# The memory's 1/rms row read back four steps later, and the memory's four parts split in the first four merged tiles instead of every second one

## The chip, the cores and the metric

The kernel runs on one core of a Trainium2 chip. The metric is the time of one execution on the device in microseconds (us), lower is better. The core's engines work side by side, each through its own queue in order: PE (TensorE, matmuls; its weight loads, PEld, overlap them), DVE (VectorE), ACT (ScalarE), POOL (GpSimd, which also issues some DMAs) and SP (SyncE, which only issues DMAs). They wait for one another through semaphores, and an instruction that waits holds up all that is queued behind it on its engine.

## The reference

One layer of a hybrid decoder over x of 512 tokens by 1024 channels, in float32, with 256 fixed memory tokens, cut to what matters here:

```
h = rms_norm(x);  proj = h @ w_in        # q, k, v | u, gate_b, gate_c | g_a, g_b
o_a = stick_breaking_attention(q, k, v)  # 8 heads of 64, causal
y_b = gate_b * causal_depthwise_conv(gate_c * u)
merged = sigmoid(g_a) * (o_a @ w_branch_a) + sigmoid(g_b) * (y_b @ w_branch_b)
x = x + merged @ w_mix_out
x = x + memory_cross_attention(rms_norm(x), rms_norm(mem), w_mem_q, w_mem_kv, w_mem_o)
x = x + (silu(gate) * up) @ w_ffn_out    # gate, up = rms_norm(x) @ w_ffn_in
out = rms_norm(x)
```

The change touches how `rms_norm(mem)` is made. Each memory token is scaled by its own 1/rms (256 numbers) and each channel by the gain `norm_mem_kv`.

## The kernel before

**Form of the work.** Activations are kept transposed, 128 channels on the partitions and 512 tokens along the free dimension, in 8 tiles. Every float32 operand of a matmul is split into a high part (a cast to fp32r) and a low part (the value minus that cast), and a product is three matmuls, high by high, high by low and low by high (`mm3`, lines 154 to 156). So each 128x1024 weight tile (`load_w`, lines 136 to 151) is loaded by SP into one of four buffers `wr`, cast by ACT to `wh` (line 149) and subtracted by DVE to `wl` (line 150). The same is done to activations (`split`, lines 168 to 178: the cast on ACT at line 172, the rest on DVE at line 174). A product over 1024 channels is 24 matmuls into one of two PSUM banks of the pool `pmm`; the next product but one needs the same bank, and so waits until DVE has read it.

**The stages around the change.** (1) The values are projected. (2) A loop of 17 turns (lines 553 to 573) does the attention of 4 head pairs p by 4 key tiles kt = 3, 2, 1, 0, so turn i is step (p, kt) = (i // 4, 3 - i % 4). In turn i PE does one or two projections out of a list `fill`, the scores of step i+1 (`scores`, midway in a projection), the weights of step i (`weights`) and the values of step i-1 (`values`). Within the scores of a step, ACT and DVE make the softplus `e`, POOL masks its diagonal block (`causal`, the affine select at line 402), and `lsplit` splits it into two tiles `l` (cast at line 416, rest at line 417). Within the weights, PE adds the running sums of the earlier key tiles onto the bank `z` (line 480) and the own step's sums (line 483, it reads both tiles `l`), ACT exponentiates `z` into `a` (line 485), POOL masks `a` (line 402 again), and DVE splits `a` into `ah` and `al` (lines 489 and 490). At the end of a head pair (kt = 0) ACT and DVE join its output `ot` (lines 510 and 511). (3) The merged tiles, m = 0 to 7 (lines 608 to 632): two gate projections, each read by DVE with line 353, two branch products `br` of 12 matmuls each read by line 625, and the split of the merged tile into `mh` and `ml`. (4) The memory's keys `km` and values `vm` (lines 635 to 663), the output projection with the residual, the cross-attention, the FFN.

**The memory.** In turns 1, 3, 5 and 7 four pieces of the memory are squared and summed. In turn 9 `mem_factors` (lines 528 to 537) makes the 1/rms `rm` of the 256 tokens, POOL writes it to DRAM (`rmd`, line 534), and POOL reads it back as a row broadcast to all partitions (`rmb`, line 536). `rmb` is first used by the keys (line 641), in stage 4. The memory itself, transposed, is split in four parts of 256 channels by `mem_split` (lines 596 to 606): SP loads a part `mk` (line 516), ACT makes two tiles `mgh` of 128x256 (line 603) and DVE two tiles `mgl` (line 604). The parts use the pool `xpool` of 8 buffers, which the residual tiles `x` (line 697) use after them. `mem_split` is called in the merged tiles m = 0, 2, 4 and 6.

**Other work at the same time.** From the merged tile m = 1 on, POOL forms sums of FFN weights (`weight_sums`, lines 579 to 590: loads `pre`, adds with line 587, stores `sums`).

**What sets the order.** The program is recorded in the order of the Python code and a scheduler orders the instructions of each engine, so that the queues differ somewhat from the code. `after(i, earlier)` ties an instruction behind earlier ones in that order only; it adds no wait on the chip. `exps` is the list of ACT's exponentials, so `exps[-1:]` in turn i is the one that the weights of the turn before issued last.

Of the kernel before, what the change touches and what calls it, by code (L numbers as in the profile page):

```python
# [8 lines left out]
F32 = mybir.dt.float32  # L9
# [4 lines left out]
P = 128  # L14
D = 1024
S = 512
KD = D // P
# [4 lines left out]
MEM = 256  # L22
# [6 lines left out]
EPS = 1e-6  # L29
MEM_AT = (1, 3, 5, 7)  # L30
MEAN_AT = 9
EARLY = 2
WARM = 8
FIRST = 4
# [9 lines left out]
def hybrid_layer(ctx: ExitStack, tc: tile.TileContext, xT_d, memT_d, mem_d, cols_d, wv_d, win_d,  # L44
                 wbr_d, wmix_d, wmq_d, wmk_d, wmv_d, wmo_d, wfi_d, wfo_d, gfin_d, out):
    nc = tc.nc

    cpool = ctx.enter_context(tc.tile_pool(name="cpool", bufs=1))
# [14 lines left out]
    def nm(s):  # L63
        count[0] += 1
        return f"{s}{count[0]}"

    def unit(s, cols=512):
        return upool.tile([P, cols], F32R, tag="u", name=nm(s), padded_shape=[P, 512])
# [34 lines left out]
    exps, casts, lead, lows, loads = [], [], [], [], []  # L103

    def after(i, earlier):
        for e in earlier:
            tc.add_manual_dep(i.ins, e.ins.name, mybir.DependencyInfo(
                mybir.DependencyClass.NoSync, mybir.DependencyReason.DATA), reason="order")
# [7 lines left out]
    def rstd_of(var, n, s, tables=()):  # L116

        def new(t):
            return tmp(t, n) if n > TT else spool.tile([P, n], F32, tag=t, name=nm(t))

        v, y, a = new("rv"), new("ry"), new("ra")
        r = cpool.tile([P, n], F32, tag=s, name=nm(s))
        after(nc.scalar.activation(y, var, AF.Ln, bias=eps_t), tables)
        nc.vector.tensor_scalar(out=v, in0=var, scalar1=EPS, scalar2=None, op0=ALU.add)
        exps.append(nc.scalar.activation(y, y, AF.Exp, scale=-0.5))
        nc.vector.tensor_tensor(out=a, in0=y, in1=y, op=ALU.mult)
        nc.vector.scalar_tensor_tensor(out=a, in0=a, scalar=-0.5, in1=v, op0=ALU.mult,
                                       op1=ALU.mult)
        nc.vector.scalar_tensor_tensor(out=r, in0=a, scalar=1.5, in1=y, op0=ALU.add, op1=ALU.mult)
        return r  # L130
# [171 lines left out]
    def settle_behind(*last):  # L302
        while urgent or behind:
            (urgent or behind).pop(0)(*last)
# [123 lines left out]
    def scores(p, kt):  # L428
        c0, n = span(kt)
        keys = slice(kt * P, (kt + 1) * P)  # L430
        zs[p, kt] = []
        for hs in heads_of(kt):
            bank = ztile("z")
            zs[p, kt].append(bank)
            for i, h in enumerate(hs):
                for part in range(2):
                    nc.tensor.matmul(bank[:, i * n:(i + 1) * n], ks[p][h][:, keys],
                                     qs[p][h][part][:, c0:], start=i + part == 0, stop=part == 1,
                                     skip_group_check=True)
        for hs, bank in zip(heads_of(kt), zs[p, kt]):  # L440
            w = len(hs) * n
            z = bank[:, :w]
            e = tmp("e")[:, :w]
            nc.scalar.activation(e, z, AF.Abs)
            nc.scalar.activation(e, e, AF.Exp, scale=-1.0)
            nc.scalar.activation(e, e, AF.Ln, bias=1.0)
            nc.vector.scalar_tensor_tensor(out=e, in0=z, scalar=0.0, in1=e, op0=ALU.max,
                                           op1=ALU.add)
            causal(by_head(e, n))
            urgent.append(lambda *last, e=e, hs=hs: fails(p, kt, hs, e, n, last))  # L450
# [21 lines left out]
    def weights(p, kt):  # L472
        c0, n = span(kt)
        av[p, kt] = {}
        for hs, bank in zip(heads_of(kt), zs[p, kt]):
            w = len(hs) * n
            z = bank[:, :w]
            if kt < TT - 1:
                for part in carried(p, kt, hs):
                    nc.tensor.matmul(by_head(z, n)[:, :, P:], neg1, part, start=False, stop=False,  # L480
                                     skip_group_check=True)
            for part in sp[p, kt, hs]:
                nc.tensor.matmul(z, negtri, part, start=False, stop=True, skip_group_check=True)
            a = tmp("a")[:, :w]
            exps.append(nc.scalar.activation(a, z, AF.Exp))
            causal(by_head(a, n))
            ah, al = unit("ah")[:, :w], unit("al")[:, :w]
            r = r0[:, kt:kt + 1]
            nc.vector.tensor_scalar(out=ah, in0=a, scalar1=r, scalar2=None, op0=ALU.mult)
            als.append(nc.vector.scalar_tensor_tensor(out=al, in0=a, scalar=r, in1=f(ah),  # L490
                                                      op0=ALU.mult, op1=ALU.subtract))
            for h in hs:
                av[p, kt][h] = part_of((ah, al), hs, (h,), n)
# [21 lines left out]
    def load_mem(k2, t):  # L515
        nc.sync.dma_start(t, memT_d[2 * k2 * P:(2 * k2 + 2) * P, :].rearrange("(j p) t -> p j t",
                                                                              p=P))
# [3 lines left out]
    def mem_square(i):  # L521

        h, t = divmod(i, MT)
        mk = f(unit("mk"))
        nc.sync.dma_start(mk, mem_d[t, :, h * 512:(h + 1) * 512])
        nc.scalar.activation(mk, mk, AF.Square, scale=D ** -0.5, accum_out=ms[:, i:i + 1])

    def mem_factors():

        var = spool.tile([P, MT], F32, tag="mv", name="mv", bufs=1)  # L530
        nc.vector.tensor_tensor(out=var, in0=ms[:, :MT], in1=ms[:, MT:], op=ALU.add)
        rm = rstd_of(var, MT, "rm")
        d = dpool.tile([1, MEM], F32, tag="rm", name="rmd")
        nc.gpsimd.dma_start(d.rearrange("o (t p) -> p (o t)", p=P), rm)
        rmb = cpool.tile([P, MEM], F32, tag="rmb", name="rmb")
        nc.gpsimd.dma_start(rmb, d.broadcast_to([P, MEM]))
        return rm, rmb

    fill = []
    for p in range(TT):  # L540
        if p + 1 < TT:
            fill += [(qk_part, p + 1, 0), (qk_part, p + 1, 1)]
        fill += [(conv, p, i) for i in range(3)]
    for m in range(EARLY):
        fill += [(gate, m, 0), (gate, m, 1)]
# [7 lines left out]
    for i in range(len(steps) + 1):  # L553
        if i in MEM_AT:
            mem_square(MEM_AT.index(i))
        if i == MEAN_AT:
            rm, rmb = mem_factors()
        some = []
        while fill and (i == len(steps) or len(some) < (2 if steps[i][1] == 1 else 1)):
            some.append(fill.pop(0))  # L560
        if i + 1 < len(steps):
            to = lambda: scores(*steps[i + 1])
            if len(some) == 1:
                midway.append(to)
            else:
                some.insert(len(some) // 2, (to,))
        for g, *args in some:
            g(*args)
        if i < len(steps):
            weights(*steps[i])  # L570
        if i > 0:
            values(*steps[i - 1])
        settle_behind(*exps[-1:], *joined[-1:])
# [22 lines left out]
    def mem_split(k2):  # L596
        mk = xpool.tile([P, 2, MEM], F32, tag="x", name=nm("mk"))
        load_mem(k2, mk)
        his, los = unit("mgh"), unit("mgl")
        for j in range(2):  # L600
            k = 2 * k2 + j
            hi, lo = (u[:, j * MEM:(j + 1) * MEM] for u in (his, los))
            nc.scalar.activation(hi, mk[:, j, :], AF.Copy, scale=g_kv[:, k:k + 1])
            nc.vector.scalar_tensor_tensor(out=lo, in0=mk[:, j, :], scalar=g_kv[:, k:k + 1],
                                           in1=f(hi), op0=ALU.mult, op1=ALU.subtract)
            mg.append((hi, lo))
# [3 lines left out]
    for m in range(KD):  # L610
        sig = []
        for j in range(2):
            if (m, j) not in gates:
                gate(m, j)
            t = gates.pop((m, j))
            sigmoid = nc.scalar.activation(t, t, AF.Sigmoid)
            after(sigmoid, exps[-2:])
            sig.append(t)
        w = load_w(wbr_d[m])
        for j in (1, 0):  # L620
            if m == 0 and j == 0:
                gate(EARLY, 0)
            ps = mmtile("br")
            gemm(ps, w, (oT, yb)[j], 4 * j)
            nc.vector.tensor_tensor(out=sig[j], in0=ps, in1=sig[j], op=ALU.mult)
        nc.vector.tensor_tensor(out=sig[0], in0=sig[0], in1=sig[1], op=ALU.add)
        if m < KD - 1:
            merged.append(split(sig[0], "m"))
        if m == SUMS_AT:
            weight_sums(range(SUMS_FIRST), merged[m][0])  # L630
        if m % 2 == 0:
            mem_split(m // 2)


    km = []
# [796 lines left out]
```

## Time and profile before

| what | value |
| --- | --- |
| median of 3 runs | 852.82 us (852.49 to 852.87) |
| the profiled execution's own time | 852.06 us |
| its span, from the first to the last instruction | 850.4 us |
| mean granted TensorE clock | 0.996 of full speed |
| busy: PE, DVE, ACT, POOL | 99%, 77%, 53%, 18% of the span |

A profile is one execution. Rows of a timeline start with the start and the duration in us, then engine, line, operation, what is written and read (buffer numbers left out) and the shape; in square brackets stand the idle time of the engine just before and what ended it. Durations of matmuls overlap, so their pace is read from start to start. A busy PE need not be at full speed: the column PEclk of the windows view is the clock that the throttle granted.

### The profile page before, as it was taken

What the parts mean: (1) busy time and instruction counts of PE and PEld (TensorE: products, weight loads), DVE (VectorE), ACT (ScalarE), POOL (GpSimd) and SP (SyncE); (2) the same over time, 40 slices, a digit from 0 to 9 for tenths busy, and PEclk for the clock granted to TensorE, in tenths of its full rate; (3) what the DMA queues carried; (4) which work ended last, traced back from release to release, by engine and by line L of the source; (5) the groups of instructions that cost most, each with busy time, mean ns of one, the idle gap of its engine ahead of it and who ended that gap; (6) DMA issues with size and microseconds to landing.
All of it is one profiled execution on the core that took longest, in us unless ns stands there. A gap on an engine that the chain in (4) does not pass through costs nothing.

```text
span 850.4 us, 12675 instructions
## 1 busy us (share of the span) xinstructions
PE 839.1 (99%) x4779; PEld 739.7 (87%) x4779; DVE 651.5 (77%) x1037; ACT 453.5 (53%) x806; POOL 155.1 (18%) x165
## 2 busy tenths in 40 slices
PE   9999998999999999999999999999999999999996
PEld 7888887888888889888888889999999999988885
DVE  7778878885766686578555688888888888899886
ACT  7566766565333254534444565655555555666654
POOL 0011121110465650065000010211111110000301
PEclk9999999999999999999999999999999999999999
DMA  8452453225587765566441324776776773465552
GB/s 298 149 168 99 124 109 97 75 75 173 210 307 291 291 250 185 173 239 237 131 124 49 88 74 142 191 187 175 183 188 177 190 191 91 145 219 205 177 183 99
DMA packets 51359, 143.73 MB, mean 169 GB/s; under 512 B 5761, under 2 KB 7041, under 8 KB 48482
## 3 DMA queue, kind: packets, MB, share of 16 engines
q1 hardware_dynamic: 41650, 107.89, 38.2%
q0 software_dynamic: 9360, 34.75, 15.6%
q8 instruction: 37, 0.61, 0.3%
q10 hardware_dynamic: 288, 0.28, 0.1%
q14 instruction: 24, 0.20, 0.1%
HBM read 125.20 MB, written 13.64 MB: 163 GB/s over the span
## 4 chain that ended last, share of the span: by engine, by line
PE 97%; DVE 1%; issue 1%; ACT 0%; POOL 0%; DVEq 0%; POOLq 0%
PE z L856 15%; PE p L1125 12%; PE y L856 7%; PE pr L154 7%; PE pr L155 7%; PE pr L156 7%; PE v L856 4%; PE r L154 3%; PE r L156 3%; PE r L155 3%; PE v L272 3%; PE mq L154 2%; PE mq L156 2%; PE mq L155 2%; PE br L154 2%; PE br L155 2%
## 5 line engine op out<-in xcount | busy, mean ns | idle before, releaser
L149 ACT CAST wh<-wr 128x1024 fp32r<-128x1024 f32 x84 | 88.0, 1052 | 159.2 <-issue 66.1
L150 DVE TENSOR_TENSOR wl<-wr,wh 128x1024 fp32r<-128x1024 f32 x84 | 111.5, 1330 | 37.9 <-ACT wh L149 37.6
L154 PE MATMUL pr<-xgh,wh 128*128 128x512 f32 x288 | 113.4, 394 | 0.0
L155 PE MATMUL pr<-xgl,wh 128*128 128x512 f32 x288 | 112.8, 392 | 0.0
L156 PE MATMUL pr<-xgh,wl 128*128 128x512 f32 x288 | 112.7, 391 | 0.0
L587 POOL TENSOR_TENSOR pre<-pre 128x512 f32<-128x512 f32 x44 | 71.2, 1622 | 31.1 <-DMA pre<-in_w_ffn_out_dram 28.8
L825 POOL DMA_DIRECT2D ws<-in_w_ffn_in_dram x22 | 26.6, 1209 | 256.6 <-DVE wf L846 123.5
L856 PE MATMUL z<-xdh,wf 128*128 128x256 f32 x352 | 70.4, 283 | 0.0
L156 PEld LDWEIGHTS pr<-xgh,wl 128*128 128x128 f32 x288 | 54.4, 189 | 11.7
L154 PEld LDWEIGHTS pr<-xgh,wh 128*128 128x128 f32 x288 | 54.6, 189 | 10.8
L155 PEld LDWEIGHTS pr<-xgl,wh 128*128 128x128 f32 x288 | 54.5, 189 | 10.5
L877 ACT COPY sa<-z 128x256 f32<-128x256 f32 x44 | 16.4, 372 | 81.5 <-PE z L856 81.5
L856 PEld LDWEIGHTS z<-xdh,wf 128*128 128x128 f32 x352 | 58.0, 192 | 0.0
L846 DVE TENSOR_TENSOR wf<-s,wf 128x512 fp32r<-128x512 f32 x44 | 30.4, 691 | 25.7 <-ACT wf L845 25.3
L856 PE MATMUL z<-xdl,wf 128*128 128x256 f32 x176 | 49.8, 283 | 0.0
L937 DVE TENSOR_TENSOR wl<-wr,wh 128x1024 fp32r<-128x1024 f32 x33 | 41.0, 1242 | 4.8 <-ACT wh L1004 4.7
L1004 ACT CAST wh<-wr 128x1024 fp32r<-128x1024 f32 x33 | 34.6, 1050 | 5.5 <-PE xt L1210 2.8
L856 PE MATMUL v<-xoh,wf 128*128 128x256 f32 x176 | 35.4, 283 | 0.0
L856 PE MATMUL y<-xch,wf 128*128 128x256 f32 x176 | 35.4, 283 | 0.0
L856 PE MATMUL z<-xf,wf 128*128 128x256 f32 x264 | 35.4, 283 | 0.0
L856 PE MATMUL z<-xch,wf 128*128 128x256 f32 x176 | 35.3, 283 | 0.0
L856 PE MATMUL y<-xoh,wf 128*128 128x256 f32 x176 | 35.3, 283 | 0.0
(346 smaller groups left out, 2389.4 us busy)
## 6 DMA issues: line engine op xcount, KB each, us to landing
wr<-in_w_in_dram SPq DMA_DIRECT2D x36, 512.0 KB, 3.4
pre<-in_w_ffn_out_dram POOLq DMA_DIRECT2D x11, 1024.0 KB, 8.0
sums<-pre POOLq DMA_DIRECT2D x11, 1024.0 KB, 4.8
ws<-in_w_ffn_in_dram SPq DMA_DIRECT2D x22, 512.0 KB, 3.7
wg<-in_w_ffn_in_dram SPq DMA_DIRECT2D x22, 512.0 KB, 4.7
ws<-in_w_ffn_in_dram POOLq DMA_DIRECT2D x22, 512.0 KB, 6.1
wr<-sums SPq DMA_DIRECT2D x22, 512.0 KB, 3.9
wr<-in_w_ffn_out_dram SPq DMA_DIRECT2D x16, 512.0 KB, 3.6
```

Of the source, the lines that this page charges most:

```text
L149: after(nc.scalar.copy(h2, raw), lead[-1:])
L150: lows.append(nc.vector.tensor_tensor(out=l2, in0=raw, in1=f(h2), op=ALU.subtract))
L154: nc.tensor.matmul(ps, a[0], b[0], start=start, stop=False, **kw)
L155: nc.tensor.matmul(ps, a[0], b[1], start=False, stop=False, **kw)
L156: nc.tensor.matmul(ps, a[1], b[0], start=False, stop=stop, **kw)
L587: nc.gpsimd.tensor_tensor(out=t[:, a, :], in0=t[:, a, :], in1=t[:, b, :], op=ALU.add)
L825: nc.gpsimd.dma_start(s13, a[:, 0:4:3, :], accum_op=ALU.add)
L846: nc.vector.tensor_tensor(out=w[:, 1, :], in0=raw, in1=f(w[:, 0, :]), op=ALU.subtract)
L856: nc.tensor.matmul(ps[:, :HS], a, b, start=i < 3 and k == 0 and j == 0, stop=k == KP - 1 and j == 2, skip_group_check=True)
L937: nc.vector.tensor_tensor(out=lo, in0=src, in1=f(hi), op=ALU.subtract)
L1004: nc.scalar.copy(hi, raw)
L1125: nc.tensor.matmul(res[i][s2], a[:, ts], b, start=j == 0 and n == 0, stop=n == 2 and j == (BEHIND - 1 if (i, s2) == (5, 1) else NJ - 1))
```

## The change

The read-back of `rmd` into `rmb` leaves `mem_factors` and is issued in turn 13, tied behind the last exponential of turn 12. `mem_split` is called in the merged tiles m = 0, 1, 2 and 3. Both parts are kept as they are in what they compute. The short name of the change also speaks of a running sum in two parts of 128 rows; no line of the diff touches a running sum.

```diff
+ROW_AT = 13
...
         nc.gpsimd.dma_start(d.rearrange("o (t p) -> p (o t)", p=P), rm)
-        rmb = cpool.tile([P, MEM], F32, tag="rmb", name="rmb")
-        nc.gpsimd.dma_start(rmb, d.broadcast_to([P, MEM]))
-        return rm, rmb
+        return rm, d
...
         if i == MEAN_AT:
-            rm, rmb = mem_factors()
+            rm, rmd = mem_factors()
+        if i == ROW_AT:
+            rmb = cpool.tile([P, MEM], F32, tag="rmb", name="rmb")
+            after(nc.gpsimd.dma_start(rmb, rmd.broadcast_to([P, MEM])), exps[-1:])
...
-        if m % 2 == 0:
-            mem_split(m // 2)
+        if m < KD // 2:
+            mem_split(m)
```

How the queues stand before and after the change is shown at three places; a row is a line of the kernel, the operation and what it writes and reads, and the lines of the changed kernel are one or two higher. PE's own queue holds the same instructions in the same order. First POOL, in the attention of the third head pair (p = 2): `e` and `a` are the masks of softplus and weights. Before:

```order
L402 AFFINE_SELECT a_1259<-a_1259 128x128
L534 DMA rmd<-rm_1374 128x2x1
L402 AFFINE_SELECT e_1310<-e_1310 128x2x128
L536 DMA rmb<-rmd 128x256
L402 AFFINE_SELECT a_1332<-a_1332 128x256
L402 AFFINE_SELECT e_1410<-e_1410 128x128
```

The same place in the changed kernel:

```order
L403 AFFINE_SELECT a_1259<-a_1259 128x128
L535 DMA rmd<-rm_1374 128x2x1
L403 AFFINE_SELECT e_1310<-e_1310 128x2x128
L403 AFFINE_SELECT a_1332<-a_1332 128x256
L403 AFFINE_SELECT e_1408<-e_1408 128x128
```

The read-back no longer stands between the mask of `e` and the mask of `a`. It stands at the same place of the fourth head pair (p = 3), again in POOL's queue of the changed kernel:

```order
L403 AFFINE_SELECT a_1646<-a_1646 128x128
L403 AFFINE_SELECT a_1657<-a_1657 128x128
L403 AFFINE_SELECT e_1696<-e_1696 128x2x128
L559 DMA rmb<-rmd 128x256
L403 AFFINE_SELECT a_1721<-a_1721 128x256
L403 AFFINE_SELECT e_1780<-e_1780 128x128
```

It was moved past 12 masks, and waits for the same store of `rmd` as before.

Second DVE in the merged tiles 1 and 2, from the split of merged tile 1 (`ml_2196`) to the read of the next gate. Before:

```order
L626 TENSOR_TENSOR g_1995<-g_1995,g_2054 128x512
L150 TENSOR_TENSOR wl_2384<-wr_2381,wh_2383 128x1024
L174 TENSOR_TENSOR ml_2196<-g_1995,mh_2195 128x512
L353 TENSOR_TENSOR g_2297<-pr_2272,r0b_363 128x512
L150 TENSOR_TENSOR wl_2418<-wr_2415,wh_2417 128x1024
```

In the changed kernel:

```order
L628 TENSOR_TENSOR g_1995<-g_1995,g_2054 128x512
L151 TENSOR_TENSOR wl_2392<-wr_2389,wh_2391 128x1024
L175 TENSOR_TENSOR ml_2196<-g_1995,mh_2195 128x512
L606 SCALAR_TENSOR_TENSOR mgl_2268<-mk_2265,gcol,mgh_2267 128x256 x2
L354 TENSOR_TENSOR g_2305<-pr_2280,r0b_363 128x512
L151 TENSOR_TENSOR wl_2426<-wr_2423,wh_2425 128x1024
```

A pair of `mgl` now stands ahead of the gate's read; the same holds after the split of merged tile 3.

Third DVE in the merged tiles 6 and 7, where `ml_2780` before and `ml_2788` now split merged tile 6. Before:

```order
L353 TENSOR_TENSOR g_2822<-pr_2797,r0b_363 128x512
L150 TENSOR_TENSOR wl_2938<-wr_2935,wh_2937 128x1024
L174 TENSOR_TENSOR ml_2780<-g_2707,mh_2779 128x512
L604 SCALAR_TENSOR_TENSOR mgl_2786<-mk_2783,gcol,mgh_2785 128x256 x2
L353 TENSOR_TENSOR g_2856<-pr_2831,r0b_363 128x512
L150 TENSOR_TENSOR wl_2973<-wr_2970,wh_2972 128x1024
```

In the changed kernel:

```order
L354 TENSOR_TENSOR g_2822<-pr_2797,r0b_363 128x512
L151 TENSOR_TENSOR wl_2938<-wr_2935,wh_2937 128x1024
L175 TENSOR_TENSOR ml_2681<-g_2608,mh_2680 128x512
L175 TENSOR_TENSOR ml_2788<-g_2715,mh_2787 128x512
L354 TENSOR_TENSOR g_2856<-pr_2831,r0b_363 128x512
L151 TENSOR_TENSOR wl_2973<-wr_2970,wh_2972 128x1024
```

The pair of `mgl` is gone from there, and the scheduler has moved the split of merged tile 5 (`ml_2681`) down to this place.

On ACT the pairs of `mgh` moved with the pairs of `mgl`. On SP the loads of the parts `mk` stand side by side, one weight load is now behind the third of them and not ahead of it, and the loads of the last three residual tiles `x`, which take over buffers of the parts, stand earlier: by two, six and ten weight loads.

## The prediction

> **What bounds the kernel now.** I read the page's engine totals first (busy us, share of the span, instructions).
>
> ```profile
> PE 839.1 (99%) x4779; PEld 739.7 (87%) x4779; DVE 651.5 (77%) x1037; ACT 453.5 (53%) x806; POOL 155.1 (18%) x165
> ```
>
> PE is busy for 99% of the span and so the bound from end to end; a change that leaves PE's matmuls alone can only win what PE waits, or what PE does at less than full clock. The second view is the waits of PE alone (line, what it waited for, total us, times, longest).
>
> ```profile
> PE z L483 <- DVE l L417: 2.4, 1, 2.4
> PE warm L232 <- DVE neg L91: 1.4, 1, 1.4
> PE br L154 <- DVE g L353: 0.3, 1, 0.3
> ```
>
> Three waits in the whole span; the one for `neg` is the start and is not touched. The third view is the windows around the first wait (length, then busy us and count of each engine; the 1.00 or 0.50 behind POOL's is the granted clock).
>
> ```profile
> 7.20:130.60 123.40, 123.40 (x579) 103.66 (x577) 98.51 (x161) 80.38 (x149) 16.84 (x33) 1.00 0.51 152
> 130.66:133.01 2.35, 0.00 (x0) 0.00 (x0) 2.25 (x5) 0.74 (x2) 0.00 (x0) 1.00 0.82 206
> 133.44:136.88 3.44, 3.44 (x12) 2.86 (x11) 3.23 (x6) 3.44 (x9) 0.08 (x1) 0.50 0.35 81
> 137.00:846.00 709.00, 705.86 (x4177) 628.41 (x4175) 543.39 (x858) 364.48 (x643) 136.97 (x123) 1.00 0.55 172
> ```
>
> The clock is full everywhere between 7.2 and 846 us except in the 3.44 us right behind this wait, where it is 0.50. So the wait costs more than its 2.35 us.
>
> The fourth view says why PE waited: POOL's timeline.
>
> ```profile
> 120.92 0.73 POOL L534 DMA_DIRECT2D rmd<-rm  x1 [3.39 <-DVE rm L129]
> 122.90 0.40 POOL L402 TENSOR_SCALAR_AFFINE_SELECT e<-e 128x256 f32<-128x256 f32 x1 [1.25 <-DVE e L447]
> 129.13 0.57 POOL L536 DMA_DIRECT2D rmb<-rmd  x1 [5.84 <-DMA rmd<-rm]
> 129.72 0.42 POOL L402 TENSOR_SCALAR_AFFINE_SELECT a<-a 128x256 f32<-128x256 f32 x1
> ```
>
> POOL stood 5.84 us in front of the read-back until the store of `rmd` had landed, and the mask of `a` stood behind it. ACT's and DVE's timelines give what that held.
>
> ```profile
> 123.58 0.38 ACT L485 ACTIVATE a<-z 128x256 f32<-128x256 f32 x1
> ```
>
> ```profile
> 123.71 1.23 DVE L150 TENSOR_TENSOR wl<-wr,wh 128x1024 fp32r<-128x1024 f32 x1 [0.17 <-ACT wh L149]
> 130.17 0.35 DVE L489 TENSOR_SCALAR ah<-a,r 128x256 fp32r<-128x256 f32 x1 [5.23 <-POOL a L402]
> ...
> 132.26 0.69 DVE L417 TENSOR_TENSOR l<-e,l 128x512 fp32r<-128x512 f32 x1
> ```
>
> `a` was ready at 123.58 + 0.38 = 123.96, but masked only at 130.14. DVE idled 5.23 us for it, with `l`, which has nothing to do with the memory, queued behind `ah`; and PE waited for `l`.
>
> **The read-back, moved four turns on.** Its price is read from start to start on PE, against the same step of the next head pair, which has the same matmuls and no wait.
>
> ```profile
> 130.04 0.40 PE L480 MATMUL z<-l,neg 128*128 128x256 f32 x2
> 130.27 0.39 PE L483 MATMUL z<-l,negtri 128*128 128x512 f32 x1
> 133.01 0.50 PE L483 MATMUL z<-l,negtri 128*128 128x512 f32 x1 [2.35 <-DVE l L417]
> ...
> 136.99 0.39 PE L155 MATMUL pr<-xgl,wh 128*128 128x512 f32 x1
> ```
>
> ```profile
> 170.48 0.40 PE L480 MATMUL z<-l,neg 128*128 128x256 f32 x2
> ...
> 173.24 0.39 PE L155 MATMUL pr<-xgl,wh 128*128 128x512 f32 x1
> ```
>
> From the first `z` of line 480 to the eighth projection matmul it took 136.99 - 130.04 = 6.95 us here and 173.24 - 170.48 = 2.76 us there. The difference, **4.19 us**, is the wait (2.35 us), the slow stretch (half of 3.44 us, 1.72), and the drained pipeline (about 0.1).
>
> Does the wait go altogether, and what is late next? Without the read-back the mask of `a` can run at 124.0 and end by 124.5; then DVE's 1.23 us `wl`, which ends at 124.94, is the later. From the start of `ah` to the end of `l` DVE needs 132.95 - 130.17 = 2.78 us, so `l` would be done at 127.7. PE needs it one matmul after 130.27, at 130.50. That is 2.8 us to spare, so I count the whole 4.19 us. Bounds: nothing, if DVE should lose those 2.8 us and the wait's length again elsewhere; at most 4.19, since PE at full pace has no more to give here.
>
> In its new place the read-back waits for a store that landed some 35 us earlier, so only its issue counts, 0.57 us. It stands between the masks of `e` and `a` of the next head pair; the row is that of `a`:
>
> ```profile
> 164.46 0.51 POOL L402 TENSOR_SCALAR_AFFINE_SELECT a<-a 128x256 f32<-128x256 f32 x1 [0.73 <-ACT a L485]
> ```
>
> POOL is idle there for 0.73 us, which holds the 0.57. If the issue took the 0.73 of the store's, the mask would be late by under 0.1 us, and the step has about the time to spare that I have just worked out for its twin. I take 0, between 0 and 0.1. The row is first read by the keys, behind all eight merged tiles. The store itself stays where it was, and the mask of `e` behind it.
>
> **The memory's parts, moved to tiles 0 to 3.** What goes is the third wait. The rows are DVE's and PE's in merged tile 7.
>
> ```profile
> 300.09 1.78 DVE L174 TENSOR_TENSOR ml<-g,mh 128x512 fp32r<-128x512 f32 x1
> 301.80 3.37 DVE L604 SCALAR_TENSOR_TENSOR mgl<-mk,gcol,mgh 128x256 fp32r<-128x256 f32 x2
> 305.09 0.68 DVE L353 TENSOR_TENSOR g<-pr,r0b 128x512 f32<-128x512 f32 x1
> ```
>
> ```profile
> 305.11 0.39 PE L156 MATMUL br<-yh,wl 128*128 128x512 f32 x1
> 305.82 0.50 PE L154 MATMUL br<-oh,wh 128*128 128x512 f32 x1 [0.32 <-DVE g L353]
> 306.16 0.40 PE L155 MATMUL br<-ol,wh 128*128 128x512 f32 x1
> ```
>
> The gate's bank is read only after the pair of `mgl`, and the second `br` product needs that bank. At the pace of 0.23 us two matmuls take 0.46; here they took 306.16 - 305.11 = 1.05, so this costs **0.59 us**, with no fall of the clock. In the changed queue the split of tile 5 takes the pair's place. At tile 6's own pace (301.80 - 300.09 = 1.71 us, start to start) two of them end at 303.5, and the gate's read is done by 304.2, 1.1 us before PE wants the bank at 305.34. I count 0.59, between 0 (the read as late as now) and 0.59.
>
> What comes: pairs of `mgl` and `mgh` in tiles 1 and 3. DVE's rows: the pair of tile 0, the split of tile 1 with the gate's read behind it, and the same read behind the split of tile 3.
>
> ```profile
> 213.41 0.88 DVE L604 SCALAR_TENSOR_TENSOR mgl<-mk,gcol,mgh 128x256 fp32r<-128x256 f32 x2
> ...
> 218.25 0.68 DVE L174 TENSOR_TENSOR ml<-g,mh 128x512 fp32r<-128x512 f32 x1
> 221.22 0.69 DVE L353 TENSOR_TENSOR g<-pr,r0b 128x512 f32<-128x512 f32 x1 [2.29 <-PE pr L156]
> ...
> 248.42 0.69 DVE L353 TENSOR_TENSOR g<-pr,r0b 128x512 f32<-128x512 f32 x1 [2.29 <-PE pr L156]
> ```
>
> A pair of `mgl` takes 0.88 us in tile 0 and 3.37 us in tile 6. Where DVE is undisturbed `ml` takes 0.68 us, in tile 6 1.78; tile 1 is of the first kind, and DVE idles 2.29 us in both new places, so I take 0.9 us inside that: cost 0. At the other end, 3.37 us overhang by 1.1, and the gate's read has a further 12 matmuls less itself, 12 x 0.23 - 0.69 = 2.0 us, before PE waits: still 0. ACT, busy for 53%, makes the pair of `mgh` ahead of it, and PE's table has no wait for ACT: 0 too. On SP, `x` loads that stand earlier wait for a pair of `mgl` and hold the weight loads behind; the first wants tile 1's pair, due at 219.9:
>
> ```profile
> 218.36 0.33 SPq L141 DMA_DIRECT2D wr<-in_w_branch_dram  x1
> 223.37 7.67 SPq L141 DMA_DIRECT2D wr<-in_w_in_dram  x2
> ```
>
> The next weight load leaves at 223.37 anyhow, 3.5 us later, so this too costs 0. The description's running sum is in no line of the diff and gets no term.
>
> **The sum.** 4.19 + 0.59 = 4.78 us. The profiled execution took 852.06 us around its span, 0.76 below the median of the runs; its own time would become 847.28, and against the median the sum gives 852.82 - 4.78 = **848.0 us**. Faster or slower means by over 0.2%, 1.7 us, about what a measurement of this kernel can tell from no change.
>
> **The rivals.**
> The slow stretch isn't the wait's. The rows say 2.35 us without a matmul, and half clock from 0.43 us after it. If the stretch has another cause it stays, 1.72 us of the gain are lost, and the time is 849.8. For it: a wait this short need not be what halves a clock for 3.44 us. Against it: from 7.2 to 846 us no other stretch is slow. Chance 0.06. [...]
>
> The wait comes back shorter, since DVE is late by something other than `ah` (its join `ot` waits for ACT, for one). With a wait of about 1 us and no fall of the clock, as the 0.32 us one had none: 849.0. The 2.8 us to spare speak against it. Chance 0.07.
>
> The change doesn't do what it says on the path: `l` is late by its own chain, or the 4.19 us come back where PE catches up with loads. Then only the 0.59 stay, 852.2. Against it: the table of PE's waits has no wait for a load or a cast, in the whole span. Chance 0.05.
>
> Slower: the pairs in tiles 1 and 3. If what slows DVE in tile 6 (I take it to be POOL's sums, which run at that time) should fall on them and the `ml` ahead (1.71 + 3.37 in place of 0.6 + 0.9, 3.6 us more), the overhang is 1.3 us, under the 2.0 allowed; it decides from 2.3 + 2.0 = 4.3 us more on. With a wait like the first one in both tiles, 2 x 4.19 - 4.78 = 3.6 us are lost, 856.4. Against it: 2.29 us of idle time in both places, and in tile 1 the undisturbed 0.68. Chance 0.05.
>
> **The numbers.** The forecast, both waits gone, has 0.77. Faster: 0.77 + 0.06 + 0.07 = 0.90; same 0.05; slower 0.05. The range reaches from 847.2, the sum on the profiled execution's own time, to 849.9, over the first two rivals.
>
> **What would show it.** In the changed profile PE's waits list the start alone; the clock is full from 7 to 840 us; POOL's read-back waits for nothing and DVE's `ah` for its mask at most a few tenths; `l` of the third head pair ends over 2 us before PE's line 483; the gate's read in tile 7 begins by 304 less the 4.2 us gained. I am wrong if PE has a wait of over 1 us anywhere from 120 to 310, or a stretch at half clock without one.

## The result and the profile after

| | median us | runs | against before (95% interval) |
| --- | --- | --- | --- |
| before | 852.87 | 5, 852.49 to 853.45 | |
| after | 846.50 | 5, 846.21 to 846.96 | 0.9925 (0.9911 to 0.9940) |

The change makes the kernel 6.4 us faster, 0.75%. The forecast was 848.0 us, from 847.2 to 849.9: the sign is right, the gain was put too low, and the time lies below the range. The profiled execution of after took 846.34 us (852.06 before), with a span of 844.6.

First the engine totals of after, then the waits of PE alone.

```profile
PE 835.9 (99%) x4779; PEld 737.6 (87%) x4779; DVE 648.7 (77%) x1037; ACT 453.4 (54%) x806; POOL 156.3 (19%) x165
```

```profile
PE warm L233 <- DVE neg L92: 1.4, 1, 1.4
PE v L273 <- DVE wvh L242: 0.2, 1, 0.2
```

The same 4779 matmuls are busy for 3.2 us less, and the waits in the attention and in merged tile 7 are gone. Only the start and a 0.2 us wait in the values' projection are left. The windows of after show what became of the clock, in one stretch from where it is first full to near the end.

```profile
4.28:840.50 836.22, 832.96 (x4774) 735.28 (x4772) 647.65 (x1031) 451.71 (x805) 155.23 (x156) 1.00 0.55 170
```

It is 1.00 throughout. (At 840.54 us, with PE's work done, it falls to half for the rest of the span.) Now the chain that the prediction went through. POOL's timeline of after, at the old and at the new place of the read-back:

```profile
120.02 0.73 POOL L535 DMA_DIRECT2D rmd<-rm  x1 [3.39 <-DVE rm L130]
121.99 0.40 POOL L403 TENSOR_SCALAR_AFFINE_SELECT e<-e 128x256 f32<-128x256 f32 x1 [1.24 <-DVE e L448]
123.17 1.11 POOL L403 TENSOR_SCALAR_AFFINE_SELECT a<-a 128x256 f32<-128x256 f32 x1 [0.78 <-ACT a L486]
...
158.66 0.57 POOL L559 DMA_DIRECT2D rmb<-rmd  x1
159.34 0.50 POOL L403 TENSOR_SCALAR_AFFINE_SELECT a<-a 128x256 f32<-128x256 f32 x1
```

The mask of `a` runs as soon as ACT has made `a`, where it stood 5.84 us before; and four turns on the read-back has no bracket behind it, so it waits for nothing. DVE's timeline of after behind the mask, and PE's at the matmul that waited:

```profile
124.32 0.35 DVE L490 TENSOR_SCALAR ah<-a,r 128x256 fp32r<-128x256 f32 x1 [0.30 <-POOL a L403]
...
126.42 0.69 DVE L418 TENSOR_TENSOR l<-e,l 128x512 fp32r<-128x512 f32 x1
```

```profile
129.13 0.40 PE L481 MATMUL z<-l,neg 128*128 128x256 f32 x2
129.36 0.62 PE L484 MATMUL z<-l,negtri 128*128 128x512 f32 x2
...
131.89 0.39 PE L156 MATMUL pr<-xgl,wh 128*128 128x512 f32 x1
```

`ah` idles 0.30 us in place of 5.23; `l` is done at 127.11, 2.5 us before the second matmul of line 484 wants it at 129.59. From the first `z` to the eighth projection matmul it is 131.89 - 129.13 = 2.76 us, the 2.76 of the next head pair, where it was 6.95. The first `z` itself comes at 129.13 and not at 130.04: 0.91 us were won ahead of anything that the change touches, at the start, where the clock of after was full from 4.28 us on and that of before from 7.14. PE's first matmuls of the values show it, before and then after: four of them took 2.04 us and 1.17 us.

```profile
5.03 2.04 PE L272 MATMUL v<-wvh,xgh 128*128 128x512 f32 x4
```

```profile
5.01 1.17 PE L273 MATMUL v<-wvh,xgh 128*128 128x512 f32 x4 [0.20 <-DVE wvh L242]
```

DVE's timeline of after in the merged tiles 1, 3 and 7:

```profile
213.72 0.88 DVE L606 SCALAR_TENSOR_TENSOR mgl<-mk,gcol,mgh 128x256 fp32r<-128x256 f32 x2
216.09 0.69 DVE L354 TENSOR_TENSOR g<-pr,r0b 128x512 f32<-128x512 f32 x1 [1.49 <-PE pr L157]
...
240.92 0.88 DVE L606 SCALAR_TENSOR_TENSOR mgl<-mk,gcol,mgh 128x256 fp32r<-128x256 f32 x2
243.29 0.69 DVE L354 TENSOR_TENSOR g<-pr,r0b 128x512 f32<-128x512 f32 x1 [1.49 <-PE pr L157]
...
294.29 1.28 DVE L175 TENSOR_TENSOR ml<-g,mh 128x512 fp32r<-128x512 f32 x2
297.69 0.69 DVE L354 TENSOR_TENSOR g<-pr,r0b 128x512 f32<-128x512 f32 x1 [2.11 <-PE pr L157]
```

The pairs of `mgl` in tiles 1 and 3 take the 0.88 us that the prediction gave them, out of 2.29 us of idle time, and 1.49 are left. In tile 7 the gate's read waits for PE again, with 2.11 us of its own to spare.

Every sign that the prediction named is there, then, and the two profiled executions differ by what it counted and by the start, which it didn't: 4.19 (the wait and the slow stretch) + 0.59 (tile 7) + 0.91 (the start) = 5.69 of 852.06 - 846.34 = 5.72 us. What went wrong is not seen in this pair of profiles. The medians differ by 6.37, and it had to be found out which of these terms belong to the change and which to the executions that were profiled.

### The profile page after: what moved, and what is told of

Its sections match the earlier page's. It is cut to its first block, busy times and chain, and to the rows that moved or that the text cites. A ratio compares the mean times of both kernels' runs of the same rounds, so it can differ in the third digit from the quotient of the medians.

```text
span 844.6 us, 12676 instructions
## 1 busy us (share of the span) xinstructions
PE 835.9 (99%) x4779; PEld 737.6 (87%) x4779; DVE 648.7 (77%) x1037; ACT 453.4 (54%) x806; POOL 156.3 (19%) x165
## 4 chain that ended last, share of the span: by engine, by line
PE 99%; DMA 0%; DVE 0%; ACT 0%; issue 0%; DVEq 0%; SPq 0%
PE z L858 15%; PE p L1127 12%; PE pr L155 8%; PE pr L156 8%; PE pr L157 8%; PE y L858 8%; PE v L858 4%; PE r L156 3%; PE r L155 3%; PE r L157 3%; PE v L273 3%; PE mq L155 2%; PE mq L157 2%; PE mq L156 2%; PE br L156 2%; PE br L155 2%
## 5 line engine op out<-in xcount | busy, mean ns | idle before, releaser
L151 DVE TENSOR_TENSOR wl<-wr,wh 128x1024 fp32r<-128x1024 f32 x84 | 115.6, 1378 | 38.3 <-ACT wh L150 38.2
L939 DVE TENSOR_TENSOR wl<-wr,wh 128x1024 fp32r<-128x1024 f32 x33 | 41.0, 1242 | 4.7 <-ACT wh L1006 4.6
```

What stands on the lines that cost most here:

```text
L151: lows.append(nc.vector.tensor_tensor(out=l2, in0=raw, in1=f(h2), op=ALU.subtract))
L939: nc.vector.tensor_tensor(out=lo, in0=src, in1=f(hi), op=ALU.subtract)
```

## The experiments

The kernels ran in three series, each with the kernel before beside it on the same chip, 23, 21 and 23 times. Its medians there were 852.07, 851.96 and 852.01, its single executions 848.98 to 854.76 us. All five executions of before in the result (852.49 to 853.45) lie above these medians; beside its own series the change wins less than in the result, 851.96 - 846.57 = 5.39 us.

**The read-back alone.** The changed kernel with the parts of the memory as before.

```diff
-        if m < KD // 2:
-            mem_split(m)
+        if m % 2 == 0:
+            mem_split(m // 2)
```

> Only the read-back moves to turn 13; the memory's parts are split as before. Theory A (the wait for l costs what the profiled execution shows, 4.2 us, and the other 1.5 us of the measured 6.4 are chance of single executions): 852.87 - 4.2 = 848.7 us. Theory B (the wait costs more in the usual execution than in the profiled one, by about 1.5 us, since the stretch at half clock behind it is longer there): 847.1 us. Theory C (the split of the parts wins more than its 0.6 us): 848.7 us here and the rest in the other half. All three: no wait of PE for l in the profile, the 0.3 us wait for the gate's read stays.

Measured: 846.58 us (6 runs, 846.22 to 847.67), 0.9940 of before (0.9922 to 0.9958). PE's waits and DVE's timeline in tile 7 of this kernel:

```profile
PE warm L233 <- DVE neg L92: 1.4, 1, 1.4
```

```profile
294.56 1.78 DVE L175 TENSOR_TENSOR ml<-g,mh 128x512 fp32r<-128x512 f32 x1
296.26 2.94 DVE L606 SCALAR_TENSOR_TENSOR mgl<-mk,gcol,mgh 128x256 fp32r<-128x256 f32 x2
299.12 0.68 DVE L354 TENSOR_TENSOR g<-pr,r0b 128x512 f32<-128x512 f32 x1
```

The read-back is the whole gain: 852.07 - 846.58 = 5.49 us, where the sum had 4.19, and nearest to theory B. The pair of `mgl` stands in front of the gate's read as before, and is slow as before (2.94 us against 3.37), but PE has no wait for `g`, which all three theories expected to stay.

**The parts alone.** The kernel before with `mem_split(m)` in the merged tiles 0 to 3, the second half of the diff.

> Only the memory's parts move to the tiles 0 to 3; the read-back stays in turn 9. Theories A and B: 852.87 - 0.6 = 852.3 us, the wait for l and a stretch at half clock behind it in the profile, no wait for the gate's read. Theory C: about 850.8 us.

Measured: 851.46 us (12 runs, 849.41 to 853.85), 0.9998 (0.9983 to 1.0012): no effect that this measurement can tell, though its interval is wide enough to hide 0.6 us. Its PE waits:

```profile
PE z L483 <- DVE l L417: 3.3, 1, 3.3
PE warm L232 <- DVE neg L91: 1.4, 1, 1.4
```

Here PE waited longest of all, 3.35 us, and the windows view has one stretch at full clock, right through the wait:

```profile
5.69:845.37 839.68, 832.32 (x4771) 734.95 (x4769) 644.32 (x1029) 450.35 (x803) 154.26 (x156) 1.00 0.54 169
```

This was not expected by any theory: the same wait, and longer, with no half clock behind it. (Only the end of the span, from 845.37 us on, is at half clock, as in after.)

**The kernel before, unaltered, twice more.**

> The kernel before, unchanged, to see how its executions differ. Theory A: executions spread around 852.9 us with one stretch of 3.4 us at half clock behind the wait in each, and differ only by where the clock becomes full at the start. Theory B: in executions of 852.8 us and more the stretch behind the wait is longer than 3.4 us, or the mean granted clock is lower than the 0.996 of the first profile (852.06 us) by some 0.001 to 0.002.

> The kernel before, unaltered, for one more profile of the same wait. Grid theory: an idle of 2.3 to 3.4 us before the scores of the second-half head pair, and behind it no half clock, one window or two, as the largest idle within one window is below 1.92 us, or over 2.17 us; the half clock lasts until a window of the grid was wholly busy; the span is longer by 0, 1.7 or up to 3.4 us accordingly. Theory of the prediction: 2.35 us and one window in every execution.

Measured: 852.41 us (12 runs, 850.03 to 854.64), 1.0006 (0.9993 to 1.0019), and 852.71 (8 runs, 849.41 to 852.96), 1.0000 (0.9982 to 1.0019). PE's waits and POOL's read-back in the profile of the first, then of the second:

```profile
PE z L483 <- DVE l L417: 2.5, 1, 2.5
PE warm L232 <- DVE neg L91: 1.4, 1, 1.4
...
128.74 0.57 POOL L536 DMA_DIRECT2D rmb<-rmd  x1 [6.02 <-DMA rmd<-rm]
```

```profile
PE z L483 <- DVE l L417: 3.0, 1, 3.0
...
129.28 0.57 POOL L536 DMA_DIRECT2D rmb<-rmd  x1 [6.44 <-DMA rmd<-rm]
```

Neither has the third wait, for `g` in tile 7: of three profiles of this kernel only the first has it. And POOL stands 5.84, 6.02 and 6.44 us in them and 6.83 us in the parts alone, as the store lands, with PE's wait 2.35, 2.54, 2.95 and 3.35 us. The half clock differs more than the wait. The windows view of the first execution of before, cut where the clock changes and 3.41 us before that (length, then PE's busy time and count; the granted clock is the figure behind POOL's):

```profile
130.02:133.44 3.42, 1.07 (x7) 0.69 (x5) 3.17 (x7) 1.17 (x3) 0.12 (x1) 1.00 0.58 144
133.44:136.85 3.41, 3.41 (x12) 2.83 (x11) 3.21 (x6) 3.41 (x9) 0.05 (x1) 0.50 0.35 82
136.85:140.26 3.41, 3.41 (x17) 2.80 (x16) 3.02 (x5) 1.74 (x3) 0.86 (x3) 1.00 0.17 41
```

The second execution (before, run again), the first two windows of the third, and the parts alone, cut in the same way:

```profile
128.85:132.26 3.41, 1.24 (x7) 0.80 (x5) 2.42 (x5) 0.38 (x1) 0.88 (x2) 1.00 0.58 132
132.26:135.67 3.41, 3.05 (x9) 2.66 (x10) 3.17 (x6) 3.41 (x9) 0.00 (x0) 0.50 0.32 61
135.67:139.09 3.42, 3.42 (x9) 2.65 (x9) 3.03 (x7) 2.52 (x5) 0.90 (x3) 0.50 0.35 80
139.09:142.50 3.41, 3.41 (x16) 2.77 (x16) 3.27 (x7) 1.65 (x3) 0.00 (x0) 1.00 0.42 141
```

```profile
129.07:132.49 3.42, 1.14 (x6) 0.71 (x5) 2.11 (x5) 0.07 (x1) 0.99 (x2) 1.00 0.66 147
132.49:135.90 3.41, 2.74 (x9) 2.35 (x10) 3.17 (x6) 3.41 (x8) 0.00 (x0) 0.50 0.18 37
```

```profile
128.57:131.98 3.41, 1.49 (x8) 1.02 (x6) 1.38 (x4) 0.00 (x0) 0.99 (x2) 1.00 0.54 101
131.98:135.40 3.42, 1.99 (x11) 1.75 (x12) 3.18 (x6) 2.74 (x7) 0.00 (x0) 1.00 0.31 56
```

In all three profiles of before the clock falls 126.29 us (to 0.01) after it was first full (133.44 - 7.14, 132.26 - 5.97, 132.49 - 6.20), and it is half for 3.41 us in the first and for 6.83 and 6.82 in the others. The 126.29 us are 37 times the 3.41 of the shortest slow stretch, more closely 37 times 3.413. The fall at the end of the span fits too: in after it comes 840.54 - 4.28 = 836.26 us after the first full clock, 245 times 3.413. So the changes of the clock that these profiles show fit a grid with marks 3.413 us apart, counted from the time at which the clock is first full, which is another in each execution. The stretch between two marks is called a window here. The clock is half behind a window in which PE idled 2.35 us in the first execution, 2.17 in the second and 2.28 in the third; in the parts alone the mark at 131.98, again 126.29 us after the first full clock (5.69), cuts the wait into 1.92 and 1.43 us, and the clock stays full. In these four profiles, then, it goes with the idle inside one window and not with the length of the wait. And the clock is full again behind a window that PE was busy throughout: after one window in the first execution, and after two in the second and third, where PE stood for the first 0.36 and 0.67 us of the slow stretch. Theory A, one slow window in each execution, falls by this, and theory B's longer stretch is there.

**The read-back one mask later.** The changed kernel with one number changed; the read-back stands behind the mask of `a` and still waits for the store.

```diff
-ROW_AT = 13
+ROW_AT = 10
```

> The changed kernel with the read-back one turn later than before instead of four: POOL's queue has it behind just one more mask, that of a. Forecast of the mechanism in the prediction (not POOL's wait costs, but what stands behind it): the wait of POOL for the store stays, some 4 us, PE has no wait, and the time equals that of the changed kernel, 846.5 us within 0.3. Rival (the store's landing collides with the attention's work wherever POOL waits for it): a PE wait of 1 to 2 us and 849 us or more.

Measured: 846.96 us (6 runs, 846.83 to 847.41), 0.9944 (0.9927 to 0.9962). POOL's timeline of this kernel, and PE's waits:

```profile
123.90 1.12 POOL L403 TENSOR_SCALAR_AFFINE_SELECT a<-a 128x256 f32<-128x256 f32 x1 [0.79 <-ACT a L486]
129.48 0.57 POOL L559 DMA_DIRECT2D rmb<-rmd  x1 [4.46 <-DMA rmd<-rm]
131.71 0.28 POOL L403 TENSOR_SCALAR_AFFINE_SELECT e<-e 128x128 f32<-128x128 f32 x1 [1.66 <-DVE e L448]
```

```profile
PE warm L233 <- DVE neg L92: 1.4, 1, 1.4
```

POOL still stands 4.46 us in front of the read-back. PE has no wait from it, since the next mask in the queue has no input before 131.7. What cost the time was the mask queued behind the wait, not the wait. The median is 0.46 us above the 846.5 expected, more than the 0.3 allowed. In the profile the clock was first full at 6.69 us and the first `z` came at 129.86, 0.73 us later than in after, so the start is enough to explain it; the other executions have no profile.

**The changed kernel again, and an idle made on purpose.** If the price is the grid's, an idle of PE must have it anywhere, also where no DMA ends the wait. In the FFN stage of the changed kernel (not in the merged stage, as the expectation for 6 selects has it) a chain of selects on POOL is issued, and one added transpose on PE waits for its end; the product that follows overwrites what the transpose wrote.

```diff
+            elif (m, i) == (10, 1):
+                bank = bank_of(m, i)
+                nc.tensor.transpose(bank[:, :P], idle, ident)
+                product(bank, m, i)
...
+            if (m, i) == (10, 0):
+                for step in range(IDLE):
+                    nc.gpsimd.affine_select(out=idle, in_=idle if step else banks[m]["s"][:, :P],
+                                            compare_op=ALU.is_gt, fill=0.0, base=0,
+                                            pattern=[[1, P]], channel_multiplier=-1)
```

> The changed kernel unaltered, beside the three idles. All theories: 846.5 us, its executions within about 1 us of each other, and TensorE's clock full from the end of its start to the last slice.

> The same idle on purpose with 4 selects: 2.22 us with 6 and 4.38 with 12 make 0.36 us a select, so about 1.5 us. Grid theory: 1.5 us is below the 1.92 us that one window of 3.41 bore without a fall, wherever it lies, so no half clock in any execution: 846.6 + 1.5 = 848.1 us, spread within 1 us as without the idle. Theory of the prediction (a stretch at half clock behind every idle of 1 to 3 us): 846.6 + 1.5 + 1.8 = 849.9 us.

> The changed kernel with one idle of TensorE made on purpose in the merged stage, with no transfer in it: a chain of 6 GpSimd selects on a 128x128 tile that a transpose ahead of a bank's product waits for (about 2 us of idle; the transpose's result is overwritten by that product). Grid theory (the half clock follows when one window of a running 3.41 us grid is idle for more than about 2 us of it, between the 1.92 that had no fall and the 2.17 that had one): an idle of 2 us costs itself alone in most executions, 848.5 us, and 1.7 us more where the idle lies inside one window, so executions spread from 848.5 to 850.3. Store theory (the half clock belongs to the stretch behind the store, not to an idle): 848.5 us in every execution, no half clock, spread within 1 us. Theory of the prediction (any idle of this size is followed by one slow stretch): 846.5 + 2.0 + 1.8 = 850.3 us in every execution.

> The same with 12 selects (about 4 us of idle). Grid theory: at least 2 us of it lie in one window wherever the idle falls, so a half clock of one window follows nearly always: 846.5 + 4 + 1.7 = 852.2 us, up to 3.4 us more where the second window is idle for over 2 us as well. Store theory: 850.5 us, no half clock. Theory of the prediction: 846.5 + 4 + 1.8 = 852.3 us in every execution, one window.

> The same with 20 selects (about 6.5 us of idle). Grid theory: one window wholly idle or two idle for over 2 us each, so the clock is half already within the idle and until the window behind it has been busy: 846.5 + 6.5 + 1.7 to 3.4 = 854.7 to 856.4 us in every execution. Store theory: 853.0 us, no half clock. Theory of the prediction: 846.5 + 6.5 + 1.8 = 854.8 us.

Measured, with the changed kernel at 846.57 (5 runs, 846.22 to 847.09; 0.9937 of before, 0.9919 to 0.9954):

| selects | median us (runs, range) | over 846.57 | PE's idle in the profile | half clock in the profile |
| --- | --- | --- | --- | --- |
| 4 | 848.24 (12, 847.51 to 848.83) | 1.67 | 1.14 | none |
| 6 | 849.99 (11, 849.23 to 850.60) | 3.42 | 2.22 | none |
| 12 | 853.38 (11, 852.63 to 853.72) | 6.81 | 4.38 | 609.80 to 616.63 |
| 20 | 856.35 (5, 856.04 to 856.44) | 9.78 | 7.31 | 610.79 to 617.62 |

The 4 selects ran in the third series, the changed kernel and the other idles in the second.

The windows view at the idle of 6 selects (the window in which the idle begins and the next), at that of 12 selects from the wholly idle window on, and at that of 20 selects the whole stretch at half clock:

```profile
603.49:606.90 3.41, 3.05 (x26) 2.84 (x24) 1.93 (x4) 2.11 (x6) 2.38 (x4) 1.00 1.02 247
606.90:610.32 3.42, 1.56 (x13) 1.57 (x14) 1.60 (x3) 2.23 (x5) 1.60 (x4) 1.00 0.58 105
```

```profile
606.39:609.80 3.41, 0.00 (x0) 0.00 (x0) 1.81 (x4) 2.43 (x5) 2.93 (x8) 1.00 0.62 114
609.80:613.21 3.41, 2.60 (x12) 2.60 (x13) 0.00 (x0) 0.00 (x0) 0.62 (x3) 0.50 0.02 5
613.21:616.63 3.42, 3.42 (x18) 3.42 (x17) 2.91 (x7) 0.96 (x2) 0.00 (x0) 0.50 0.22 74
616.63:620.00 3.37, 3.37 (x31) 3.37 (x30) 1.65 (x4) 0.28 (x1) 1.00 (x1) 1.00 0.61 222
```

```profile
610.79:617.62 6.83, 3.53 (x17) 3.53 (x18) 0.45 (x2) 0.41 (x1) 2.65 (x9) 0.50 0.01 2
```

With 6 selects the mark at 606.90, as the grid has it, cuts the 2.22 us into 0.36 and 1.86, and there is no fall. With 12, one window is wholly idle, the clock is half from 609.80, and PE's busy time at half clock (from 610.61 to 616.63, 6.02 us) loses an estimated half of it, 3.01 us: with the idle that is 7.39, and the span is 852.0 - 844.9 = 7.1 longer than that of the changed kernel. With 20 the fall comes while PE still stands, so only 3.53 busy microseconds are at half clock; the sum, estimated in the same way, is 7.31 + 1.77 = 9.08, measured by the spans 9.5.

The store theory (the half clock belongs to the stretch behind the store, so an idle made on purpose costs itself alone) is out: by the idles measured it would give 851.0 and 853.9 for 12 and 20 selects, below every execution. The theory of the prediction, one slow stretch of 1.8 us behind every idle, falls on the profiles of 4 and 6 selects, which have none, and of 12, which has two windows. For 4 selects no execution (848.83 at most) comes near that theory's 849.9, and the median is 0.1 above the grid theory's 848.1.

For 6 selects the executions are less clear than the profile, whose span is 2.6 us longer than that of the changed kernel for 2.22 us of idle. Their median, 849.99, is nearer to the 850.3 of the prediction's theory than to the 848.5 that the grid theory gave most of them: seven of them (849.23 to 850.13) have a mean clock of 0.997, four (850.35 to 850.60) of 0.995 or 0.996, which fits some falls, but the two groups touch. The idle of 4 selects was shorter in its profile (1.14) than forecast (1.5). That profile is of the fastest execution, so the idle of the other eleven isn't known. The times of 4 and 6 selects alone would not decide between the theories; their profiles and those of 12 and 20 do.

## Why the prediction was right in its mechanism and wrong in its size

**Right: the chain and where it goes.** The store, the read-back, the mask of `a`, `ah`, `l`, PE: each link behaved as put, and moving the read-back by one mask is enough for PE not to wait (`ROW_AT = 10`). The read-back in its new place costs 0, the pairs in tiles 1 and 3 cost 0, and what could have been late next isn't: `l` has 2.5 us to spare against the 2.8 worked out. For the execution that was profiled the sum was right: 852.06 - 4.78 and the start's 0.91 give 846.37 us, and 846.34 was measured.

**Wrong: the step from one execution to the median.** The prediction put it as "against the median the sum gives 852.82 - 4.78". That holds only if the 4.78 us are the price of the waits in every execution, so that the 0.76 us between the profile and the median stay as they are. They don't. The median of after, 846.50, lies 0.16 from its own profile, as its executions agree within about a microsecond; what made those of before differ was in the main the term that went. The miss is 848.04 - 846.50 = 1.54 us, made of two parts: the 0.76, which did not stay, and 847.28 - 846.50 = 0.78, which is the start's 0.91 and the 0.03 that the three terms left over, less the 0.16. The 0.76 is chance in part: 852.06, the profiled execution's own time, is also the median of the 67 executions of before in the three series, and the three on record with the prediction (852.49 to 852.87) lay above it. That they were longer by the same wait is argued from the table below; they have no profile.

**The term of 4.19 us was mis-sized.** It was taken from one execution and put as the most that the wait can cost ("at most 4.19"). Measured as a difference of medians, the read-back wins 852.07 - 846.58 = 5.49 us alone and 852.07 - 846.96 = 5.11 at `ROW_AT = 10`. In the four profiles the wait is 2.35 to 3.35 us, with no, one or two windows at half clock behind it (one window is 3.41 us; the prediction's 3.44 reached a little past its end). There the price can be worked out: to the time of a kernel without the wait whose clock was first full at about the same moment (846.57 us at 5.95, 846.93 at 6.69) add the wait and half of PE's busy time at half clock. The half is an estimate from the 0.50 of the windows; by the rows of the third run of before, the 128x512 matmuls started 0.43 us apart in the slow stretch and 0.23 behind it.

| profile | sum | measured |
| --- | --- | --- |
| before, the first | 846.93 + 2.35 + 3.41 / 2 + 0.59 (tile 7) = 851.58 | 852.06 |
| before, run again | 846.57 + 2.54 + 6.47 / 2 = 852.35 | 852.38 |
| before, third run | 846.57 + 2.95 + 6.15 / 2 = 852.60 | 852.78 |
| the parts alone | 846.57 + 3.35 = 849.92 | 850.27 |

The sums come within 0.5 us. By them one and the same wait cost 4.1, 5.8, 6.0 and 3.4 us, mostly by the number of slow windows. The mean clock hints at that number in 87 executions of the kernel before. One window of 3.41 us at a clock of 0.50 takes 3.41 / 2 / 850 = 0.002 off the mean clock, and the half clock at the end of the span, where PE has no work, takes off 0.001 to 0.003 as well (2.25 us of it at `ROW_AT = 10`, 5.20 in the third run of before), so that after has 0.998 to 0.999:

| mean clock | executions | us | median | over after (846.5) |
| --- | --- | --- | --- | --- |
| 0.998 to 0.999 | 20 | 848.98 to 850.45 | 849.45 | 3.0 |
| 0.996 to 0.997 | 31 | 851.21 to 852.91 | 851.85 | 5.4 |
| 0.993 to 0.995 | 36 | 852.22 to 854.76 | 852.93 | 6.4 |

I read the rows as no window, one and two; the profiles with none, one and two have 0.998 (the parts alone), 0.996 and 0.993. The bounds between them are mine, and single executions can be on the wrong side: the 17 with 0.995 can be one window with a long end or two with a short one. By this reading the gain is 3.0 to 6.4 us by the phase, and its usual size is that of the two lower rows, 67 of 87 executions; the profile shown at the outset was of the middle one. A prediction from it could have seen a sign of this: a wait that ends 0.43 us before the clock falls says that something else than the wait sets the moment.

**The term of 0.59 us was a chance, too.** The wait for `g` was in one of three profiles of the kernel before and not in that of the read-back alone, and the parts moved by themselves win nothing that can be told (0.9998). The sharper comparison is the read-back alone, at 846.58 us, with both halves of the change, at 846.50 and 846.57: the parts add 0.1 us at most between these medians. Between 0 and 0.59 the lower bound was the better number.

**The rival on the slow stretch.** It had 0.06, and falls: the stretch goes when the wait goes, and comes with an idle made on purpose. It is true only that the wait alone does not decide it, as the parts alone have the longest wait, 3.35 us, and no stretch. Nor did the clock need a window without any matmul to fall: in the first profile of before it is half behind a window with 1.07 us of matmuls in 3.42, and in the parts alone it stays full behind one with 1.49 in 3.41.

**What stays open.** It isn't known what part of the differences between the rows of the table comes from the windows at half clock, and what from the longer wait or the start, since these executions have no profile: the first step, 2.4 us, is more than the estimated 1.7 of one window. The start moves the first `z` by up to 0.91 us in the profiles (129.13 to 130.04). Why the store lands at another time in each execution, which sets the length of the wait, isn't known. The end of a span has an idle of PE too, and in one profile it comes close to that of the parts alone. The third run of before has 3.41 - 1.47 = 1.94 us of it in the last window in which PE works, and the clock is half behind it:

```profile
842.46:845.87 3.41, 1.47 (x13) 1.26 (x11) 2.78 (x11) 2.71 (x9) 0.00 (x0) 1.00 0.75 287
845.87:849.29 3.42, 0.00 (x0) 0.00 (x0) 1.04 (x3) 0.72 (x1) 0.00 (x0) 0.50 0.64 237
```

So the clock stayed full behind 1.92 us and was half behind 1.94, as far as the modelled ends of matmuls go. Two windows do not show that there is a limit between the two, and whether the idle time decides or something that goes with it isn't known.

No version here is clearly faster than the changed kernel: it, the read-back alone and the one at `ROW_AT = 10` are at 846.50 to 846.96, and PE's waits list little but the start.

## What to carry to other kernels

A DMA that waits for another DMA on a queue shared with computing holds up what is queued behind it, as POOL's 5.84 us did here; ask what that is, and move either past the other. One mask was enough. A profile shows one draw of a wait: where the executions of a kernel spread over several microseconds, look at more than one profile before pricing the wait, and ask whether the spread itself goes with it, since the median then falls by more than the row shows. In these profiles an idle of PE of 2.2 to 3.4 us had no, one or two windows at half clock behind it (two in the second execution of before, an estimated 3.2 us lost), which fits where the grid cut it; the windows at full clock with 1.14, 1.86 and 1.92 us of idle had full clock behind them.

## What the runs showed of the hardware

- TensorE's clock fell 126.29 us after it was first full in the three profiles of before, 37 times 3.413, and 836.26 us after it in after, 245 times 3.413; where it fell behind a wait or an idle made on purpose, it was half for 3.41, 6.82 or 6.83 us. A window at full clock with 1.14, 1.86 or 1.92 us of idle time was followed by full clock, one with 1.94, 2.17, 2.28, 2.35 or 3.41 by half.
- In the five profiles with such a stretch it was full again behind the first slow window in which PE was busy throughout. Where PE still idled 0.36 us (before, run again), 0.67 (before, third run), 0.81 (12 selects) or 3.30 us (20 selects) of the first slow window, a second one followed.
- The longest idle lost less to the clock than a shorter one: an estimated 1.77 us behind 7.31 us of idle, 3.01 behind 4.38 (half of PE's busy time at half clock, 3.53 and 6.02 us).
- The start is part of the spread: the clock was first full between 4.28 and 7.14 us, and the profiled executions without the wait for `l` went from 846.34 (4.28) over 846.49 (5.52) and 846.57 (5.95) to 846.93 (6.69, `ROW_AT = 10`).
